# A copy of the scan inputs' PSUM tile, made by ScalarE and read by VectorE's rotations

## The chip, the cores and the metric

The kernel runs on one core of one Trainium2 chip. The metric is the device time of one execution in microseconds (us). The core's engines work side by side, each through its own queue of instructions in a fixed order: TensorE (PE; its weight loads are listed as PEld), VectorE (DVE), ScalarE (ACT), GpSimd (POOL) and SyncE (SP), which here only starts DMA transfers. Matrix products land in PSUM; everything else lies in SBUF. GpSimd has no operand in PSUM in this kernel.

## What is computed

One layer of a diffusion backbone, for 128 context tokens and 1024 latent tokens of width 1024: a normalised input goes through one input projection, whose columns feed attention (queries, keys, values) and a state-space layer (u). The part at stake is the state-space layer, a complex diagonal scan in two directions for 32 groups:

```python
bu_re = jnp.einsum('blgc,gpc->blgp', uf, bb_re)
bu_im = jnp.einsum('blgc,gpc->blgp', uf, bb_im)
bu_re = bu_re.at[:, edge].add(ab_re * h0r - ab_im * h0i)
bu_im = bu_im.at[:, edge].add(ab_re * h0i + ab_im * h0r)
_, _, h_re, h_im = lax.associative_scan(
    _complex_affine_combine, (a_re, a_im, bu_re, bu_im), axis=1, reverse=reverse)
y = (jnp.einsum('blgp,gcp->blgc', h_re, c_re[dr])
     - jnp.einsum('blgp,gcp->blgc', h_im, c_im[dr]))
```

A gated unit, the output projection and a feed-forward part follow.

## The kernel before

**Stages.** Modulation and normalisation of the input come first, to about 180 us. Then the input projection runs through 63 steps (`STEPS`), each a chunk of 256 columns for one tile of 128 tokens: 24 products of 128x256 into one tile `ps_in` (`win_mm`, L463 to L465). `ps_in` has three buffers. The step behind it empties it (`win_evac`): ScalarE with a copy (L483) or, for the queries and keys of the latent tokens, VectorE with the rotary products (L488 to L495: L488, L493 and L494 read `ps_in` in PSUM, L495 adds two SBUF tiles). VectorE also makes the low part of each weight tile (L272) behind ScalarE's cast (L271).

**The scans lie beside the projection.** The order of all instructions is written out by hand: between the products of a step, a generator (`side`) is moved on by one part, which puts instructions of the scans into all queues. `ssm_pipe` handles four groups at a time, a batch; there are eight batches (Q = 0 to 7), started some two or three steps apart, so that two or three of them overlap. In the traces they run from about 228 to 376 us.

**One batch.** Tables of sines and cosines `E` are made by ScalarE and VectorE (L926 to L959; L928 and L940 add a bias, L930, L936 and L943 are VectorE's steps between). `U` holds the transposed inputs. Then, for a direction d, `rot_in(d)`: TensorE makes the scan inputs in `pS` (L977, 16 products; one tile of two PSUM banks with a single buffer), and VectorE rotates them with the tables: `rotate` is one product of 128x576 into `tA` (L967) and two of 128x288 into `tB` (L968, L969). GpSimd adds the two into `St` (L983) and adds the start state to one column (L985). `rot_out(d)`: VectorE scans (L1001, two instructions, with the decay in `dr`, made by ScalarE at L993) into `Ht` in SBUF, rotates `Ht` back with the same `rotate`, and GpSimd adds the result into `Hp` in four instructions (L1008) and writes its edge columns (L1012 to L1018). TensorE reads `Hp` in the output products `yc` and `yl` (L1043 to L1050), two steps after the second `rot_out`.

**What sets the order around the change.** In the queue of each engine `rot_in(0)` comes one part ahead of `rot_in(1)`, and this ahead of `rot_out(0)`; `rot_out(1)` is in the part behind. With the batches interleaved, `rot_in(0)` of the next batch stands on VectorE right behind `rot_out(1)` of the one before in most batches. `tA`, `tB` and `St` have two buffers each, `pS`, `Ht` and `dr` one for their use. So the products into the next `pS` wait until the last read of the present one.

**After the scans** the projection goes on alone (TensorE), the keys are transposed, and attention begins at some 430 us.

Of the kernel before, what the change touches and what calls it, by code (L numbers as in the profile page):

```python
# [34 lines left out]
CH = 8  # L35
# [22 lines left out]
def tile_hybrid_step(  # L58
# [86 lines left out]
    def rsqrt1s(pl, cols):  # L145
        """The inverse root of some columns, divided by RS."""
        ts = []
        for ss, scale, tag in cols:
            v, y, f = [pl.tile([P, 1], F32, tag=tag + n, name=tag + n) for n in "vyf"]
            yi = pl.tile([P, 1], I32, tag=tag + "i", name=tag + "i")  # L150
            ts.append([v, y, f, yi, yi.bitcast(F32)])
        for (v, y, f, yi, cur), (ss, scale, tag) in zip(ts, cols):
            if scale is None:
                V.tensor_scalar(v, ss[:, 0:1], ss[:, 1:2], EPS, ALU.add, ALU.add)
            else:
                V.tensor_scalar(v, ss, scale, EPS, ALU.mult, ALU.add)  # L156
        for v, y, f, yi, cur in ts:
            V.tensor_single_scalar(yi, v.bitcast(I32), 1, op=ALU.logical_shift_right)
        for v, y, f, yi, cur in ts:
            V.tensor_scalar(yi, yi, -1, 0x5F3759DF, ALU.mult, ALU.add)  # L160
        for c in (-3.0, -12.0, -768.0):
            for v, y, f, yi, cur in ts:
                V.tensor_scalar(f, cur, cur, v, ALU.mult, ALU.mult)  # L163
            for x in ts:
                v, y, f, yi, cur = x
                V.scalar_tensor_tensor(y, f, c, cur, ALU.add, ALU.mult)  # L166
                x[4] = y
        return [x[1] for x in ts]
# [18 lines left out]

    # ------------------------------------------------------------- pools for the first part
    pst_es, pst = pool("pst", space=PSUM)
# [17 lines left out]

    # ------------------------------------------------------------- loads
    wm_raw = {}
# [6 lines left out]
    def load_wm0(j, n):  # L216
        """Half of a quarter of the first shift's (n even) or scale's columns."""
        if j % 2 == 0:
            w = p0.tile([P, 4, NW], F32, tag=f"x{4 + n}", name=f"wm0{j}{n}")
        else:  # L220
            if n % 2 == 0:
                wm_raw[j, n // 2] = p0w.tile([P, 2, 4, NW], F32, tag=f"w{n // 2}", name=f"wm0{j}{n}")
            w = wm_raw[j, n // 2][:, n % 2]
        wm_raw[j, n // 2, n % 2] = w
        c = n % 2 * D + j * NW
        DMA.dma_start(w, wmod[:, n // 2 * 4:n // 2 * 4 + 4, c:c + NW])
# [86 lines left out]
    load_wm0(1, 3)  # L313
    # ------------------------------------------------------------- modulation, statistics, normalised input
    def mod_mm(ps, c0, nq, k):
# [18 lines left out]

    # ------------------------------------------------------------- statistics of the rows
    TG = [(0, 4), (4, 8), (8, 9)]
# [52 lines left out]

    # ------------------------------------------------------------- input and output maps, state on the partitions  # L390
    prm = pb.tile([P, NQ, 4, 8, GC], F32, name="prm")
# [56 lines left out]

    # ------------------------------------------------------------- input projection
    u_sb = [su.tile([P, 8, CH, GC], F32, name=f"u_sb{o}") for o in range(4)]  # L450
# [53 lines left out]

    # ------------------------------------------------------------- the start

# [12 lines left out]
    def mod_out(j):  # L519
        """Shifts and scales of two blocks of channels."""  # L520
        rows = mod_rows(psm0.pop(j))
        pm = ps_t("pm0")[:, 0:P]
        PE.transpose(pm, rows, ident)
        pmv = pm.rearrange("p (i b r) -> p i r b", i=2, r=32)
        s = slice(2 * j, 2 * j + 2)
        for i, n in enumerate(("sh1", "sc1")):
            V.tensor_tensor(mods[n][:, :, s], pmv[:, i, 0:2, :],
                            bT[:, None, 8 * i + 2 * j:8 * i + 2 * j + 2].to_broadcast([P, 2, 2]), ALU.add)
        V.tensor_tensor(mods["sc1"][:, :, s], mods["sc1"][:, :, s], gT[:, 0, None, s].to_broadcast([P, 2, 2]), ALU.mult)
# [18 lines left out]

    # small things
    ones2 = pp.tile([P, 2, NS], F32, name="ones2")  # L550
# [305 lines left out]

    # ------------------------------------------------------------- maps of the scans, four groups of a direction at a time
    def after(f):
# [57 lines left out]

    # ------------------------------------------------------------- scans, four groups at a time
    def ssm_pipe(sp, Q):
# [44 lines left out]
        def tmp(n):  # L963
            return sp.tile([P, 2, 2, NS], F32, tag=n, bufs=2, name=n)
        def rotate(x, d, s):
            tA, tB = tmp("tA"), tmp("tB")
            V.tensor_mul(tA, x, tab(d, 0)[:, None].to_broadcast([P, 2, 2, NS]))  # L967
            V.tensor_mul(tB[:, s], x[:, 1 - s], tab(d, 1))  # L968
            V.scalar_tensor_tensor(tB[:, 1 - s], x[:, s], -1.0, tab(d, 1), ALU.mult, ALU.mult)  # L969
            return tA, tB  # L970
        def rot_in(d):
# [8 lines left out]
            pSv = pS[:, :, 0:2 * NS].rearrange("p r (u c) -> p r u c", u=2)  # L980
            tA, tB = rotate(pSv, d, 0)
            St = tmp("St")
            G.tensor_tensor(St, tA, tB, ALU.add)  # L983
            c0 = 0 if d == 0 else NCH - 1
# [111 lines left out]
    class Pipe:  # L1096
        """Staggered generators: a new one every `every` steps, each moved on once a step."""

# [15 lines left out]

    # the rest of the modulation, a quarter of its columns at a time
    MSEC = (2048, 3072, 4096, 5120)
# [54 lines left out]

    # ------------------------------------------------------------- keys
    kvd = {}
# [41 lines left out]

    # ------------------------------------------------------------- gated unit
    zsp = {}
# [91 lines left out]

    # ------------------------------------------------------------- the projection, with the rest beside it  # L1310
    tm_es = None
# [34 lines left out]
    p1_es.close()  # L1346
    # ------------------------------------------------------------- attention
    def rsqrt_pool(pl, ss, n, scale, tag, bufs=1, split=False):
# [188 lines left out]

    # ------------------------------------------------------------- gated unit
    gl_es, gl = pool("gl", side="left")
# [17 lines left out]

    # the context's queries go beside the unit's products
    def ctx(m):
# [117 lines left out]

    # ------------------------------------------------------------- output projection, second norm
    mx_load(order[1])
# [24 lines left out]

    # quarters of the second part's input: half of the tokens, half of its columns, half of that half of tokens
    quart = [{n: slot(f"r{4 * b + i}", dt=F32) for i, n in enumerate(("A11", "A12", "A21", "A22"))} for b in range(2)]
# [73 lines left out]

    # weights of the second part's inputs: quarters, their sums, split
    raw, wop = {}, {}
# [178 lines left out]

    # ------------------------------------------------------------- feed-forward: gate and up parts
    psf_es, psf_ = pool("psf", space=PSUM)
# [13 lines left out]
    def prod(f, i, b):  # L1977
        """One of the seven products of a block, and the sums that it completes."""
        u = un.setdefault((f, b), {})
# [125 lines left out]

    # ------------------------------------------------------------- feed-forward: second product
    HEAD = 1
# [36 lines left out]

    # the seven products of a pair of rows' tiles, of columns' halves and of token tiles (q, q + 4)
    def w2_load(p):
# [5 lines left out]
    def w2_tasks(p):  # L2152
        """Sums in place and splits: rows' tiles (0, 1), columns' halves (0, 1)."""
        at = {1: (0, 0), 7: (0, 1), 2: (1, 0), 3: (1, 1), 5: (2, 0), 6: (2, 1), 4: (1, 0)}
# [68 lines left out]
    def mm2(ps, s, p, n, ix, start, stop):  # L2223
        """Passes of one product: tokens' operand ix by the rows' operand n."""
        h, l = [t[1][:, ix] if isinstance(ix, int) else t[1][:, ix[0], ix[1]] for t in g2[s]]
        w = W2[p][n][1]
        for j, (x, y) in enumerate(((h, w[:, 0, :]), (h, w[:, 1, :]), (l, w[:, 0, :]))):
            PE.matmul(ps, x, y, start=(start and j == 0), stop=(stop and j == 2))  # L2228
# [279 lines left out]
def _rope_tables():  # L2508
    """Rotary tables of the token grid (shapes alone), rows ordered as the token tiles are:
    partition p of tile j holds token p * CH + j; the sine of an axis once for both halves."""  # L2510
    tok = (np.arange(P)[:, None] * CH + np.arange(CH)[None, :])
# [30 lines left out]
```

## Time and profile before

| what | value |
|---|---|
| median of 3 runs | 1561.93 us (1559.25 to 1562.45) |
| profiled execution, span from first to last instruction | 1562.2 us |
| TensorE busy | 1451.2 us (93%) |
| VectorE busy | 1177.3 us (75%) |
| ScalarE busy | 677.4 us (43%) |
| GpSimd busy | 534.6 us (34%) |

The profile is of one execution; its span is its own time, and only what lies ahead of the first and behind the last instruction is not in it. The page's busy shares are means over stages with different limits. The table of stretches gives the same by stage, the list of waits says which engine waited for what, and the lines of a source line give the shortest, the median and the longest duration of its instructions. Durations of neighbouring instructions of VectorE overlap a little, so that starts tell more of what one costs than ends.

### The profile page before, as it was taken

The numbers are of one execution on the slowest core, as the hardware profiler recorded it, in microseconds if no ns is written. First come the engines' busy times: TensorE is split into PE (matmuls) and PEld (weight loads), VectorE is DVE, ScalarE is ACT, GpSimd is POOL, SyncE is SP. The second block draws the span as 40 slices with busy tenths as digits, with TensorE's granted clock in tenths as the row PEclk, the third lists the DMA queues.
The fourth block names the chain that finished last, engine by engine and source line by source line (L and its number), as shares of the span: only waits on it lengthen the run. The fifth ranks groups of instructions, "written<-read, shape, count | busy, mean of one in ns | idle before, by whom it ended". The sixth has DMA issues, their size and how long they took to land. (4 is left out here: it accounts for less than half of the span.)

```text
span 1562.2 us, 27432 instructions
## 1 busy us (share of the span) xinstructions
PE 1451.2 (93%) x10331; PEld 1326.9 (85%) x10331; DVE 1177.3 (75%) x2049; ACT 677.4 (43%) x1381; POOL 534.6 (34%) x656
## 2 busy tenths in 40 slices
PE   4879998989999999989879999999999999999986
PEld 3867797888989999868779999999999996888765
DVE  5579839997558888648797666666666678898988
ACT  2443255542658887536652223222322236333322
POOL 1355417774113442321440000000000017786866
PEclk9879999999999999989999999999999999999998
DMA  9329944333442111055412222222222123333325
GB/s 294 117 80 334 338 156 120 109 114 111 126 147 80 48 49 35 8 159 166 121 42 75 81 79 72 67 82 78 72 67 81 58 94 106 107 115 106 123 94 189
DMA packets 162452, 175.70 MB, mean 112 GB/s; under 512 B 18080, under 2 KB 132720, under 8 KB 162320
## 3 DMA queue, kind: packets, MB, share of 16 engines
q1 hardware_dynamic: 161392, 173.24, 34.8%
q8 instruction: 82, 1.34, 0.4%
q10 hardware_dynamic: 816, 0.57, 0.1%
q0 software_dynamic: 112, 0.13, 0.1%
q14 instruction: 50, 0.41, 0.1%
HBM read 128.70 MB, written 45.20 MB: 111 GB/s over the span
## 5 line engine op out<-in xcount | busy, mean ns | idle before, releaser
L1984 PE MATMUL m<-l,wh 128*128 128x288 f32 x1320 | 276.7, 296 | 5.5 <-DVE l L1712 4.4
L1984 PE MATMUL m<-r,wh 128*128 128x288 f32 x1144 | 241.5, 297 | 3.4 <-DVE rav L156 3.0
L1984 PEld LDWEIGHTS m<-l,wh 128*128 128x128 f32 x1320 | 215.6, 189 | 6.6 <-DVE l L1712 4.9
L1984 PE MATMUL m<-l,wl 128*128 128x288 f32 x704 | 208.4, 296 | 2.9 <-DVE wl L1801 2.9
L1984 PEld LDWEIGHTS m<-r,wh 128*128 128x128 f32 x1144 | 188.0, 189 | 4.2 <-DVE r L1712 4.0
L463 PE MATMUL ps_in<-wh,hh 128*128 128x256 f32 x576 | 179.7, 312 | 5.0 <-DVE hh L385 4.1
L465 PE MATMUL ps_in<-wh,hl 128*128 128x256 f32 x576 | 167.4, 291 | 5.5 <-DVE hl L388 5.5
L464 PE MATMUL ps_in<-wl,hh 128*128 128x256 f32 x576 | 167.3, 290 | 0.7 <-DVE wl L272 0.7
L2162 POOL TENSOR_TENSOR l<-r 128x512 f32<-128x512 f32 x2 | 3.0, 1521 | 452.8 <-DMA r<-in_w_ffn_out_dram 452.8
L1984 PE MATMUL m<-r,wl 128*128 128x288 f32 x528 | 157.1, 298 | 0.2 <-DVE wl L1801 0.2
L1800 ACT CAST wh<-raw 128x512 fp32r<-128x512 f32 x132 | 77.8, 621 | 147.4 <-DVE raw L1826 117.6
L463 PEld LDWEIGHTS ps_in<-wh,hh 128*128 128x128 f32 x576 | 114.6, 199 | 25.3 <-issue 18.9
L1984 PEld LDWEIGHTS m<-l,wl 128*128 128x128 f32 x704 | 133.1, 189 | 3.1 <-DVE wl L1801 3.1
L1801 DVE TENSOR_TENSOR wl<-raw,wh 128x512 fp32r<-128x512 f32 x132 | 93.3, 708 | 38.5 <-ACT wh L1800 38.4
L465 PEld LDWEIGHTS ps_in<-wh,hl 128*128 128x128 f32 x576 | 114.4, 199 | 6.5 <-DVE hl L388 6.4
L464 PEld LDWEIGHTS ps_in<-wl,hh 128*128 128x128 f32 x576 | 115.0, 200 | 1.1 <-DVE wl L272 1.1
L1424 DVE TENSOR_REDUCE mx<-S 128x1 f32<-128x1152 f32 (+1 forms) x72 | 88.7, 1236 | 22.1 <-PE S L1421 21.8
L1984 PEld LDWEIGHTS m<-r,wl 128*128 128x128 f32 x528 | 100.3, 190 | 0.5 <-DVE wl L1801 0.4
L2264 DVE TENSOR_TENSOR acc<-acc,fo 128x1024 f32<-128x1024 f32 (+1 forms) x77 | 82.8, 1102 | 8.4 <-PE fo L2228 8.4
L1431 ACT ACTIVATE p<-S,mx 128x1152 f32<-128x1152 f32 (+1 forms) x72 | 81.1, 1127 | 13.9 <-DVE mx L1424 10.2
L1421 PE MATMUL S<-kT,qT 128*128 128x384 f32 x384 | 83.0, 351 | 0.5 <-ACT p L1431 0.5
L1008 POOL TENSOR_TENSOR Hp<-tA,tB 64x288 f32<-64x288 f32 x64 | 61.6, 963 | 30.7 <-DVE tB L969 26.3
(550 smaller groups left out, 3535.0 us busy)
## 6 DMA issues: line engine op xcount, KB each, us to landing
wm<-in_w_mod_dram SPq DMA_DIRECT2D x48, 512.0 KB
raw<-in_w_ffn_in_dram SPq DMA_DIRECT2D x88, 256.0 KB
g_s<-u SPq DMA_DIRECT2D x88, 144.0 KB
wraw<-in_w_in_dram SPq DMA_DIRECT2D x28, 256.0 KB
r<-in_w_ffn_out_dram SPq DMA_DIRECT2D x12, 512.0 KB
l<-in_w_ffn_out_dram SPq DMA_DIRECT2D x10, 512.0 KB
mat_s<-out SPq DMA_DIRECT2D x16, 288.0 KB
omat<-mat_s SPq DMA_DIRECT2D x8, 576.0 KB
```

Of the source, the lines that this page charges most:

```text
L463: PE.matmul(ps, la, wh, start=(k == 0), stop=False)
L464: PE.matmul(ps, la, wl, start=False, stop=False)
L465: PE.matmul(ps, lb, wh, start=False, stop=(k == KD - 1))
L1008: G.tensor_tensor(H[64 * ri:64 * ri + 64, two::2, off:off + NS], tA[s, ri], tB[s, ri], ALU.add)
L1421: PE.matmul(S[:, c, 0:cw], qT[:, 2 * h + m, j, :], K[:, 2 * h + m, c * cw:(c + 1) * cw], start=(j == 0), stop=(j == 1))
L1424: V.tensor_reduce(u["mx"][:, m:m + 1], S[:, 0:nc3, 0:cw], mybir.AxisListType.XY, ALU.max, negate=True)
L1431: A.activation(p[:, 0:nc3 * cw].rearrange("p (c n) -> p c n", n=cw), u["S"][m][:, 0:nc3, 0:cw], AF.Exp, bias=u["mx"][:, m:m + 1], scale=1. ...
L1800: A.copy(h, src)
L1801: V.tensor_sub(l, src, h)
L1984: PE.matmul(ps, w[:, k, :], a[:, k, :], start=(k == 0 and j == 0), stop=(k == 3 and j == 2))
L2162: G.tensor_tensor(x(o), x(a), x(b), ALU.subtract)
L2264: V.tensor_add(a, a, x)
```

## The change

ScalarE copies `pS` into `St` in SBUF (576 elements a partition), and the three multiplications of `rotate` read `St` instead of `pS`. GpSimd's addition then writes into the same `St`, over the copy. `rotate` itself, the scan and the back rotation are as before. Lines behind it have a number higher by one.

```diff
@@ -978,8 +978,9 @@
             pSv = pS[:, :, 0:2 * NS].rearrange("p r (u c) -> p r u c", u=2)
-            tA, tB = rotate(pSv, d, 0)
             St = tmp("St")
+            A.copy(St, pSv)
+            tA, tB = rotate(St, d, 0)
             G.tensor_tensor(St, tA, tB, ALU.add)
```

The rest of the diff takes comments away and changes no instruction. Each of the 16 calls of `rot_in` puts one instruction more into ScalarE's queue, and no other instruction is added or moved. Where it stands, in ScalarE's queue at batch 1, between the decay of batch 1 (`dr`) and the steps for the tables (`f`) and the weights (`wh`); before:

```order
L993 ACTIVATE dr_3115<-ones_293,prq 128x144 [waits DVE_49]
L993 ACTIVATE dr_3115<-ones_293,prq 128x144
L928 ACTIVATE f_3067<-f_3065,magic 128x512
L271 CAST wh<-wraw 128x512 [waits DMAHW7_49]
L940 ACTIVATE f_2904<-f_2902,magic 128x512 [waits DVE_49]
L946 COPY U<-pu 128x4x128 [waits PE_49]
```

The same place of ScalarE's queue in the changed kernel:

```order
L994 ACTIVATE dr_3117<-ones_293,prq 128x144 [waits DVE_49]
L994 ACTIVATE dr_3117<-ones_293,prq 128x144
L982 COPY St<-pS 128x576 [waits PE_49,Pool_49]
L928 ACTIVATE f_3069<-f_3067,magic 128x512
L271 CAST wh<-wraw 128x512 [waits DMAHW7_49]
L982 COPY St<-pS 128x576 [waits PE_49,Pool_49]
L940 ACTIVATE f_2904<-f_2902,magic 128x512 [waits DVE_49]
```

The two copies of the batch stand behind `dr`, which waits for VectorE's last scan of the batch before, and each waits for TensorE's products into `pS`.

On TensorE, the second direction's products into `pS` of batch 1, between products of the projection; before:

```order
L463 MATMUL ps_in<-wh,hh_3_280 128x256
L464 MATMUL ps_in<-wl,hh_3_280 128x256
L465 MATMUL ps_in<-wh,hl_3_288 128x256
L977 MATMUL pS<-U,mat 64x144 [waits DVE_49,PE_49]
L977 MATMUL pS<-U,mat 64x144 x7
```

And in the changed kernel, on TensorE at the same place:

```order
L463 MATMUL ps_in<-wh,hh_3_280 128x256
L464 MATMUL ps_in<-wl,hh_3_280 128x256
L465 MATMUL ps_in<-wh,hl_3_288 128x256
L977 MATMUL pS<-U,mat 64x144 [waits Activation_49]
L977 MATMUL pS<-U,mat 64x144 x7
```

The order is the same; the products now wait for ScalarE's copy of the first direction's `pS` instead of VectorE's three reads of it. On VectorE the order is the same too, and `pS` as the first operand of L967 to L969 has become `St`.

## Rows read from the trace of the kernel before

**Rows 1.** The page, busy time: engine, us, share of the span, instructions.
```profile
PE 1451.2 (93%) x10331; PEld 1326.9 (85%) x10331; DVE 1177.3 (75%) x2049; ACT 677.4 (43%) x1381; POOL 534.6 (34%) x656
```

**Rows 2.** Busy time by stretch: us, engines, granted clock, DMA share, GB/s.
```profile
240.00:360.00 120.00, 101.95 (x970) 93.77 (x969) 114.94 (x192) 56.48 (x143) 87.49 (x123) 0.94 0.41 118
...
376.00:424.00 48.00, 47.58 (x417) 47.41 (x418) 24.65 (x62) 25.82 (x46) 4.08 (x4) 1.00 0.42 126
```

**Rows 3.** Waits, 200 to 400 us: total, times, longest one.
```profile
PE pS L977 <- DVE tB L969: 18.1, 7, 4.6
...
ACT dr L993 <- DVE Ht L1001: 12.2, 4, 4.5
...
DVE Ht L1001 <- POOL St L985: 2.6, 4, 0.7
...
DVE tA L967 <- PE pS L977: 2.2, 2, 1.5
```

**Rows 4.** Timeline of TensorE, VectorE and GpSimd at the last batch: start, duration, instruction.
```profile
357.81 1.27 PE L977 MATMUL pS<-U,mat 128*64 128x144 f32 x16 [2.48 <-DVE tB L969]
...
375.30 0.66 PE L1043 MATMUL yc<-omat,Hp 128*32 128x128 f32 x16
...
359.19 0.76 DVE L967 TENSOR_TENSOR tA<-pS,E 128x576 f32<-128x576 f32 x1 [1.53 <-PE pS L977]
...
370.50 3.80 POOL L1008 TENSOR_TENSOR Hp<-tA,tB 64x288 f32<-64x288 f32 x4 [0.47 <-DVE tB L969]
...
375.30 0.19 POOL L1018 COPY Hp<-h0s 128x4 f32<-128x4 f32 x1
```

**Rows 5.** Line L967: shortest, median, longest in ns; first and last start.
```profile
L967 DVE TENSOR_TENSOR tA<-pS,E x16: 744/748/758, 228.4 to 359.2; 128x576 f32<-128x576 f32 x16
L967 DVE TENSOR_TENSOR tA<-Ht,E x16: 757/758/1185, 236.7 to 368.4; 128x576 f32<-128x576 f32 x16
```

**Rows 6.** Line L946, ScalarE's copy out of PSUM, 226 to 372 us.
```profile
L946 ACT COPY U<-pu x7: 559/585/588, 230.1 to 341.8; 128x512 f32<-128x512 f32 x7
```

**Rows 7.** Lines L488, L495, L930 and L1008, 226 to 372 us.
```profile
L488 DVE TENSOR_TENSOR rt<-ps_in,rc x18: 409/411/420, 238.7 to 370.9; 128x256 f32<-128x256 f32 x18
...
L495 DVE TENSOR_TENSOR st<-st,rt x18: 424/1028/1053, 239.6 to 371.7; 128x256 f32<-128x256 f32 x18
...
L930 DVE SCALAR_TENSOR_TENSOR f<-f,f x6: 685/686/1289, 238.1 to 335.1; 128x512 f32<-128x512 f32 x6
...
L1008 POOL TENSOR_TENSOR Hp<-tA,tB x62: 784/886/1190, 238.3 to 371.7; 64x288 f32<-64x288 f32 x62
```

**Rows 8.** Timeline of VectorE and GpSimd, 292 to 297 us.
```profile
292.99 1.29 DVE L930 SCALAR_TENSOR_TENSOR f<-f,f 128x512 f32<-128x512 f32 x1
294.20 1.28 DVE L272 TENSOR_TENSOR wl<-wraw,wh 128x512 fp32r<-128x512 f32 x1
...
292.62 4.40 POOL L1008 TENSOR_TENSOR Hp<-tA,tB 64x288 f32<-64x288 f32 x4 [2.32 <-DVE tB L969]
```

**Rows 9.** Timeline of VectorE and GpSimd at 230 us.
```profile
230.26 1.75 DVE L943 SCALAR_TENSOR_TENSOR f<-f,f 128x512 f32<-128x512 f32 x1 [0.37 <-ACT f L940]
...
230.03 1.43 POOL L983 TENSOR_TENSOR St<-tA,tB 128x576 f32<-128x576 f32 x1 [13.63 <-ACT dr L993]
```

**Rows 10.** Timeline of VectorE and GpSimd at batch 3, 282 to 289 us.
```profile
282.06 0.75 DVE L967 TENSOR_TENSOR tA<-pS,E 128x576 f32<-128x576 f32 x1
...
283.45 1.03 DVE L936 TENSOR_TENSOR f<-f,f 128x512 f32<-128x512 f32 x1
...
285.25 1.03 DVE L495 TENSOR_TENSOR st<-st,rt 128x256 f32<-128x256 f32 x1
...
282.29 3.70 POOL L1008 TENSOR_TENSOR Hp<-tA,tB 64x288 f32<-64x288 f32 x4 [1.69 <-DVE tB L969]
...
286.58 1.42 POOL L983 TENSOR_TENSOR St<-tA,tB 128x576 f32<-128x576 f32 x1
```

**Rows 11.** Busy time of 358 to 362 us, columns as in rows 2.
```profile
358.00:362.00 4.00, 4.00 (x30) 3.73 (x28) 2.81 (x5) 0.00 (x0) 3.15 (x5) 0.60 0.42 135
```

## The prediction

> **What bounds the kernel now.** I read the page first: TensorE is busy for 93% of the span, so a change in work that VectorE and ScalarE do beside it is worth what it moves on TensorE, in its own stage [rows 1]. The scans run from about 228 to 376 us. There the table of stretches turns the picture round: between 240 and 360 us VectorE is busy for 114.9 of 120 us, TensorE for 102.0, ScalarE for 56.5, at a granted clock of 0.94; from 376 us on TensorE is busy for 47.6 of 48 and VectorE for 24.7 [rows 2]. So in the scans VectorE is late, behind them TensorE is.
>
> The list of waits says how the two hang together: seven times, 18.1 us in all, TensorE waits before the products into pS until VectorE has written tB, its last read of the pS before [rows 3]. pS has one buffer, and these are the only long waits of TensorE there. This is what the change goes for.
>
> The question is whether those 18.1 us reach the end. I followed the last batch. TensorE's output product of the eighth batch (yc, L1043) begins to take Hp at 375.30; GpSimd's last copy into that Hp starts at 375.30 and lasts 0.19; no wait is listed [rows 4]. The two arrive together, and behind that point TensorE has no gap. GpSimd's Hp follows from VectorE's last rotation (0.47 us idle until tB) [rows 4], and that from VectorE's queue, which is full. So the end moves with **VectorE's chain through the eight batches**: a TensorE that is early at the last yc only waits there. Long before, it waits elsewhere: ps_in has three buffers, which VectorE empties (L488 to L494) at fixed places of the same full queue.
>
> **The change part by part.** Removed: the 48 reads of pS by VectorE (three for each of 16 tiles). The three instructions themselves stay, in the same places. From pS tA takes 744 to 758 ns; the same instruction on Ht, which lies in SBUF, takes 757 ns at least and 758 at the median [rows 5]. For VectorE the copy is no lighter work: zero for 48 instructions, a few tenths of a us at most on the wrong side. The Trainium skill (VectorE: DVE Perf Modes, "The TRN2 errata") gives a VectorE instruction a fixed 58 cycles from SBUF and 120 from PSUM, at 0.96 GHz; by it 48 instructions would gain an estimated 3.1 us and the forecast would be 1570. The rows on the two forms of tA show none of that, so it is left out of the sum.
>
> Added on ScalarE: 16 copies of 128x576. The nearest row is its copy of 128x512 from PSUM, 585 ns [rows 6]; by elements about 0.65 us. ScalarE has half of its time free, so 10.5 us of copies are hidden, except where a copy stands between TensorE and a waiting VectorE. Behind a copy in ScalarE's queue are the bias steps of the tables (L928, L940) and the weight casts (L271), which VectorE takes up later. In batches 1, 3, 4 and 5 the first copy stands right behind the activation of dr, which itself waits for VectorE's last scan (ACT dr on Ht: 4 times, 12.2 us) [rows 3]; VectorE has three rotation instructions to do after that scan, about as long as dr and copy together, so nothing is added there. In batch 0 VectorE isn't full and waits for pS itself (2.2 us in two waits, 1.53 of them at the last batch, so 0.7 here) [rows 3, 4]: copy and hand-over come on top, **+0.8 us**.
>
> Added on VectorE, by what it now reads: **waiting for GpSimd**. The trace shows two kinds of VectorE instruction. Those with one operand in PSUM don't notice GpSimd: L488 takes 409 to 420 ns in all 18 cases [rows 7]. Those with both operands in SBUF do: L495 takes 424 ns at best and 1028 at the median; L930 and L272 right behind each other, both while GpSimd adds up Hp, take 1.29 and 1.28 us [rows 7, 8], where the least for L930 is 0.69 [rows 7]. So each instruction that meets the Hp additions is held by 0.6 us, also several in a row. Beside the longer addition of St it is 1.06: L943 takes 1.75 us there [rows 9] against a usual 0.69. The rotations of pS are of the first kind, and after the change of the second. That rotations on Ht look unharmed is because GpSimd is mostly waiting for their tB; the one that meets GpSimd takes 1185 ns, 0.43 over the median [rows 5].
>
> Batch 3 shows the place. The first direction's rotation starts at 282.06, the four Hp additions at 282.29, and until 285.99 they run beside it, L936 and L495; L936 now takes 0.34 more than the 0.69 of L930, which has its size, and L495 0.61 more than its least, 0.95 of holding in all [rows 7, 10]. After: tA starts first and is free, the two tB and L936 are held 0.6 each, and L495 meets the rest of the fourth addition, 0.2 or so: 2.0. Net +1.1. Batches 1 to 7 all have the rotation beside such additions, some with more of them left, some with less: 7 x 1.1 = **+7.7 us**. The bounds are zero (no hold) and three full holds each, 7 x 1.8 = 12.6.
>
> The second direction's rotation runs beside the addition of St (in batch 3 from 286.58 on, 1.42 us [rows 10]), and in four batches the scan behind it then waits for that St, 2.6 us in all, 0.65 each [rows 3]. One hold of 1.06 takes the place of such a wait: +0.4, four times: **+1.6 us**. In batch 7 VectorE now waits 1.53 us for pS [rows 4]; TensorE will no longer be late there, and a hold of 1.06 comes instead: **-0.5 us**. VectorE's chain: 0.8 + 7.7 + 1.6 - 0.5 = **+9.6 us**.
>
> **What TensorE makes of it.** Its waits move rather than go: VectorE's chain gets longer, TensorE's work doesn't, so it waits more than now, at ps_in and before the last yc. There is one effect behind that. After the wait of 2.48 us at 357.81 the clock granted is 0.60 in the 4 us from 358 [rows 4, 11], so most of that at the lower level (1.2 GHz): 0.4 x 4 = 1.6 us lost. Today that loss lies ahead of the tie at 375 us. After the change the last long wait is the one at the yc itself (I expect some 3 us, between the emptying of ps_in and Hp), and the loss lies behind it, on the path: **+1.6 us**. From there on TensorE's work is as before, without gaps that could take up a shift of 10 us.
>
> Sum: 9.6 + 1.6 = 11.2 us on the span of 1562.2, so 1573.4; the median of the runs, 1561.93, is the same as that span within 0.3. I forecast 1573.
>
> **The rivals.**
> 1. *The hold takes the whole instruction of GpSimd*, not 0.6 us: 0.89 (median of an Hp addition [rows 7]) and 1.42 for St [rows 10]. Then three holds for each first direction are longer by 0.29, 7 x (1.1 + 0.87) = 13.8 instead of 7.7, and five of the second by 0.36, 1.8: 7.9 us over the forecast, 1581. Against it: consecutive holds of 0.60. The Trainium skill says this (SBUF, "Who interferes with whom"): VectorE with two SBUF inputs and a GpSimd instruction that reads SBUF exclude each other, and the second waits until the first has finished. The rows agree on who is hit, not on how much. 5%.
> 2. *No hold that matters*: the rotations find gaps in GpSimd's work, or the delays fall where VectorE would have waited. Then 0.8 - 1.5 on VectorE's chain and up to 1.6 of clock: 1562 to 1564, no difference. For it: rotations on Ht are nearly all at 758 ns. 15%.
> 3. *TensorE's waits do set the end*, and the change does what it is written for: faster. All 18.1 us would give 1544. But VectorE's queue allows only its own idle time to go: 2.6 us of waits for St and 1.5 for pS [rows 3, 4], so 1558. It decides if the holds stay under those 4.1 us and batch 7 gains from an early pS. For it: the clock, 0.94 in the stage, would recover too. 9%.
> 4. *ScalarE's queue stalls VectorE*: a copy that waits for pS keeps L928, L940 or the casts back. With the 0.65 us of a copy in each of 16 places, 10 us on top: 1584. Against it: ScalarE's idle half. 3%.
>
> **How the numbers follow.** The forecast has the remaining 68%; with its bounds (holds half as large or a third larger, clock loss or none) it runs from 1566 to 1579. A range of 1561 to 1581 takes in the first and the second rival, and leaves out the third and the fourth. Slower by over 0.2% (3.1 us, about what a measurement of this kernel can tell from no change): forecast, first and fourth rival, 0.76. Faster by as much: most of the third, 0.08. The rest within it, 0.16.
>
> **What would show it.** In the profile after: tA and tB from St up to 1.3 and 1.0 us where they meet Hp, at 0.76 and 0.45 elsewhere; the wait of TensorE for tB gone from pS, and waits of the same size at ps_in (on VectorE's L494) or at yc (on GpSimd's Hp); VectorE still over 95% busy in the stage, and that stage some 10 us longer; the copies at 0.6 to 0.7 us; a granted clock near 0.5 behind the last yc. I am wrong if tA from St stays at 0.76 beside GpSimd, or if the last yc comes before 376 us.

## The result and the profile after

The changed kernel takes **1573.01 us** (median, 1572.08 to 1574.73), the kernel before 1561.56 beside it: a ratio of 1.0079, 95% interval 1.0064 to 1.0093. The forecast was 1573, slower. The profiled execution took 1574.73 us with a span of 1573.0, 10.8 us more than before. In the changed kernel the copy is L982; the lines behind it have moved down by one.

The page's busy times answer to [rows 1]: VectorE has 11 us more, ScalarE 9 (the copies), GpSimd 9 (7.4 of them in its additions and small copies beside the scans; the last section comes back to this).

```profile
PE 1455.7 (93%) x10331; PEld 1330.0 (85%) x10331; DVE 1188.3 (76%) x2049; ACT 686.7 (44%) x1397; POOL 543.2 (35%) x656
```

The same stretches as in [rows 2], with the end of the scans apart (columns: us; busy us of TensorE, its weight loads, VectorE, ScalarE, GpSimd; granted clock, DMA share, GB/s):

```profile
240.00:360.00 120.00, 101.47 (x915) 91.66 (x915) 118.91 (x178) 60.11 (x148) 87.06 (x111) 0.90 0.35 104
371.00:386.00 15.00, 10.36 (x102) 9.62 (x100) 14.72 (x27) 1.79 (x4) 11.73 (x16) 0.93 0.36 103
386.00:436.00 50.00, 49.58 (x420) 49.19 (x413) 24.45 (x62) 25.82 (x46) 4.08 (x4) 0.95 0.40 121
384.00:388.00 4.00, 2.36 (x16) 1.98 (x17) 2.44 (x6) 0.00 (x0) 1.42 (x4) 0.50 0.57 176
388.00:392.00 4.00, 4.00 (x26) 4.00 (x26) 0.00 (x0) 0.65 (x2) 0.00 (x0) 0.66 0.02 5
```

VectorE had 5 of 120 us free between 240 and 360; now it has 1. It also does less in them: 178 instructions instead of 192. Behind the scans, from 386 us on, TensorE is full again, but around the last wait, from 384 to 392 us, the granted clock is 0.50 and then 0.66.

The waits from 200 to 420 us, as in [rows 3]:

```profile
ACT dr L994 <- DVE Ht L1002: 17.9, 6, 6.3
...
PE pS L977 <- ACT St L982: 13.8, 5, 4.9
...
PE yc L1044 <- POOL Hp L1019: 6.2, 5, 2.1
...
PE ps_in L463 <- DVE st L494: 2.5, 1, 2.5
```

TensorE's 18.1 us of waits for VectorE's tB are gone by name, but 13.8 us of them have come back as waits for the copy. The first line says why: in ScalarE's queue the copy stands behind dr, and dr waits for VectorE's scan. To these come 6.2 us before yc and 2.5 before ps_in.

What VectorE pays is seen by adding up its instructions from the first rotation to the last Hp, with the same counts in both kernels. These groups are of the kernel before, 228.30 to 375.60 us (busy us and mean ns, then idle time ahead of the group):

```profile
L967 DVE TENSOR_TENSOR tA<-pS,E 128x576 f32<-128x576 f32 x16 | 12.0, 749 | 2.9 <-PE pS L977 2.2 <-ACT E L990 0.7
...
L969 DVE SCALAR_TENSOR_TENSOR tB<-pS,E 128x288 f32<-128x288 f32 x16 | 7.1, 446 | 0.0
L968 DVE TENSOR_TENSOR tB<-pS,E 128x288 f32<-128x288 f32 x16 | 7.1, 445 | 0.0
```

And these of the changed kernel, 229.60 to 385.65 us:

```profile
L967 DVE TENSOR_TENSOR tA<-St,E 128x576 f32<-128x576 f32 x16 | 14.5, 905 | 3.6 <-DMA wraw<-in_w_in_dram 2.5 <-ACT St L982 1.1
...
L969 DVE SCALAR_TENSOR_TENSOR tB<-St,E 128x288 f32<-128x288 f32 x16 | 12.1, 754 | 0.0
L968 DVE TENSOR_TENSOR tB<-St,E 128x288 f32<-128x288 f32 x16 | 12.0, 749 | 0.0
L272 DVE TENSOR_TENSOR wl<-wraw,wh 128x512 fp32r<-128x512 f32 x10 | 11.7, 1166 | 0.0
```

The 48 rotation instructions grew from 26.2 to 38.6 us, **+12.4** with rounding. The others take a part of it back: L272 10.5 to 11.7, L936 5.1 to 5.9, L943 5.9 to 5.4, L495 18.0 to 17.1, the scans' waits for St 2.6 to 0.2, together -1.8; and inside the stretch VectorE waits 1.1 us ahead of tA instead of 2.2, and no more the 0.4 us ahead of L943. From the first rotation to the last copy into Hp it is 155.6 us (229.75 to 385.39) instead of 146.9 (228.40 to 375.30).

Batch 3 shows how it happens; timeline of VectorE and GpSimd in the changed kernel, the place of [rows 10]:

```profile
284.62 0.75 DVE L967 TENSOR_TENSOR tA<-St,E 128x576 f32<-128x576 f32 x1
285.29 1.05 DVE L968 TENSOR_TENSOR tB<-St,E 128x288 f32<-128x288 f32 x1
286.26 1.05 DVE L969 SCALAR_TENSOR_TENSOR tB<-St,E 128x288 f32<-128x288 f32 x1
...
290.66 1.68 DVE L969 SCALAR_TENSOR_TENSOR tB<-St,E 128x288 f32<-128x288 f32 x1
...
284.84 4.34 POOL L1009 TENSOR_TENSOR Hp<-tA,tB 64x288 f32<-64x288 f32 x4 [1.69 <-DVE tB L969]
...
290.38 1.65 POOL L984 TENSOR_TENSOR St<-tA,tB 128x576 f32<-128x576 f32 x1
```

tA has started before GpSimd and runs at 0.75. Both tB start beside the Hp additions and take 1.05 instead of 0.45. In the second direction one tB meets the St addition and takes 1.68. In the other batches it is the same: tA at 1.35, tB at 1.05 beside Hp, 1.66 or 1.68 beside St, everything else at 0.75 to 0.80 and 0.44 to 0.47.

The end, in the timeline of TensorE and GpSimd, as [rows 4]:

```profile
381.98 0.35 PE L463 MATMUL ps_in<-wh,hh 128*128 128x256 f32 x1 [2.50 <-DVE st L494]
...
385.64 0.66 PE L1044 MATMUL yc<-omat,Hp 128*32 128x128 f32 x8 [2.14 <-POOL Hp L1019]
...
385.39 0.19 POOL L1019 COPY Hp<-h0s 128x4 f32<-128x4 f32 x1
```

The last copy into Hp starts 10.1 us later than the 375.30 of before, and TensorE, which was there on time, now waits for it. Such a difference of two times on the clock takes in where the scans began: the first products into pS end at 227.61 here, at 228.02 before, and anywhere between 222.97 and 228.02 in the ten profiles, though the code up to them is the same. Lengths from the first rotation on are free of that, and are used below.

### The profile page after: what moved, and what is told of

It is laid out like the page before. It is cut to its first block, busy times and chain, and to the rows that moved or that the text cites. A ratio compares the mean times of both kernels' runs of the same rounds, so it can differ in the third digit from the quotient of the medians.

```text
span 1573.0 us, 27458 instructions
## 1 busy us (share of the span) xinstructions
PE 1455.7 (93%) x10331; PEld 1330.0 (85%) x10331; DVE 1188.3 (76%) x2049; ACT 686.7 (44%) x1397; POOL 543.2 (35%) x656
## 5 line engine op out<-in xcount | busy, mean ns | idle before, releaser
L464 PE MATMUL ps_in<-wl,hh 128*128 128x256 f32 x576 | 166.3, 289 | 0.5 <-DVE wl L272 0.3
L463 PEld LDWEIGHTS ps_in<-wh,hh 128*128 128x128 f32 x576 | 113.7, 197 | 27.7 <-issue 21.4
L1802 DVE TENSOR_TENSOR wl<-raw,wh 128x512 fp32r<-128x512 f32 x132 | 93.4, 709 | 38.6 <-ACT wh L1801 38.5
L464 PEld LDWEIGHTS ps_in<-wl,hh 128*128 128x128 f32 x576 | 113.9, 198 | 0.9 <-DVE wl L272 0.9
L1425 DVE TENSOR_REDUCE mx<-S 128x1 f32<-128x1152 f32 (+1 forms) x72 | 88.6, 1236 | 22.0 <-PE S L1422 21.6
L2265 DVE TENSOR_TENSOR acc<-acc,fo 128x1024 f32<-128x1024 f32 (+1 forms) x77 | 82.8, 1102 | 9.2 <-PE fo L2229 9.2
L1432 ACT ACTIVATE p<-S,mx 128x1152 f32<-128x1152 f32 (+1 forms) x72 | 81.1, 1127 | 13.8 <-DVE mx L1425 10.2
```

Source lines behind the costliest of these rows:

```text
L463: PE.matmul(ps, la, wh, start=(k == 0), stop=False)
L464: PE.matmul(ps, la, wl, start=False, stop=False)
L1425: V.tensor_reduce(u["mx"][:, m:m + 1], S[:, 0:nc3, 0:cw], mybir.AxisListType.XY, ALU.max, negate=True)
L1432: A.activation(p[:, 0:nc3 * cw].rearrange("p (c n) -> p c n", n=cw), u["S"][m][:, 0:nc3, 0:cw], AF.Exp, bias=u["mx"][:, m:m + 1], scale=1. ...
L1802: V.tensor_sub(l, src, h)
L2265: V.tensor_add(a, a, x)
```

## The experiments

The **theory**: VectorE's chain sets the end of the scans, and the rotations got slower because both operands now lie in SBUF while GpSimd reads SBUF too. The **rivals**: the price is the copy itself, by ScalarE's queue or by a longer way from TensorE to VectorE; or TensorE's own waits set the end.

**The copies made, but not read.** The copy goes into St, the rotations read pS.

```diff
             St = tmp("St")
-            tA, tB = rotate(pSv, d, 0)
+            A.copy(St, pSv)
+            tA, tB = rotate(pSv, d, 0)
```

> The 16 copies of pS into St are made as in the changed kernel, but the rotations read pS as before (the copy is overwritten unread). Theory (the time comes from GpSimd holding VectorE's multiplications once both their operands lie in SBUF): 1560 to 1564, no different from before, tA and tB at 0.75 and 0.45 us everywhere, last Hp written at 375 to 376 us. Rival A (the copies themselves: ScalarE's queue and the hand-over delay VectorE's chain): 1568 or more. Rival B (an SBUF operand is slower for VectorE, GpSimd or not) gives 1562 as well and is told apart by the next two.

Measured: 1562.93 us, ratio 1.0008 (0.9996 to 1.0019), no difference, as expected; the kernel before takes 1561.31 beside it and beside the next three. From the first rotation to the last copy into Hp it is 147.5 us (227.16 to 374.68). The rotations stay at means of 753 and 446 ns. The first one waits for the copy here too, though it reads pS: 2.48 us, as in the changed kernel, until 0.03 us behind the copy's end. So 16 copies in ScalarE's queue, hand-over included, cost nothing that can be measured; the interval leaves room for 3 us.

**Only tA reads the copy**, both tB read pS.

```diff
-        def rotate(x, d, s):
+        def rotate(x, d, s, xa=None):
+            xa = x if xa is None else xa
...
-            V.tensor_mul(tA, x, tab(d, 0)[:, None].to_broadcast([P, 2, 2, NS]))
+            V.tensor_mul(tA, xa, tab(d, 0)[:, None].to_broadcast([P, 2, 2, NS]))
...
-            tA, tB = rotate(pSv, d, 0)
+            A.copy(St, pSv)
+            tA, tB = rotate(pSv, d, 0, St)
```

> Only tA reads the copy, the two tB read pS: one of three multiplications can be held, and VectorE waits for the copy as in the changed kernel. Theory: in the changed kernel tA is on average 0.16 us longer than from pS and each tB 0.30, so 16 x 0.16 = 2.5 us and 0.8 of hand-over, 1564 to 1567. Rival A (copies and hand-over): 1573, as with all three. Rival B: a third of the 11 us, spread over all 16 tA evenly (each 0.2 longer, GpSimd busy or not), 1565.

Measured: 1572.28 us, ratio 1.0059 (1.0036 to 1.0082). That is nearly the whole loss with only 4 holds, and was not what the theory expected. VectorE's groups, 227.60 to 382.05 us:

```profile
L1003 DVE TENSOR_TENSOR_SCAN Ht<-dr,St 128x288 f32<-128x288 f32 x32 | 37.8, 1220 | 5.0 <-POOL St L987 5.0
...
L968 DVE TENSOR_TENSOR tA<-St,E 128x576 f32<-128x576 f32 x16 | 14.4, 902 | 8.6 <-ACT St L983 7.2 <-POOL Hp L1010 1.4
```

The holds of tA are 2.4 us (902 against 749 ns). The larger part is idle time: 8.6 us ahead of tA and 5.0 ahead of the scans, where before had 2.9 and 2.6. Ahead of tA: here pS is freed only by the last tB, so the copy of the second direction starts late, and tA waits for TensorE and ScalarE one after the other: 2.50 us at the last batch alone, where before waits 1.53. Ahead of the scans: the four waits for St are twice as long (1.25 to 1.27 each). The second direction of batch 4, in the kernel before and in this one:

```profile
304.54 0.74 DVE L967 TENSOR_TENSOR tA<-pS,E 128x576 f32<-128x576 f32 x1
304.54 0.19 POOL L1017 COPY fin<-Hp 128x4 f32<-128x4 f32 x1
...
304.93 1.43 POOL L983 TENSOR_TENSOR St<-tA,tB 128x576 f32<-128x576 f32 x1
```

```profile
306.86 0.75 DVE L968 TENSOR_TENSOR tA<-St,E 128x576 f32<-128x576 f32 x1
306.86 0.79 POOL L1019 COPY fin<-Hp 128x4 f32<-128x4 f32 x1
...
307.85 1.42 POOL L985 TENSOR_TENSOR St<-tA,tB 128x576 f32<-128x576 f32 x1
```

Beside a tA that reads pS, GpSimd's small copy takes 0.19 us; beside one that reads St it takes 0.79, and the addition into St follows 0.99 us behind tA instead of 0.39. In the other three batches it is the same: the addition comes 0.6 us later, and the scan waits for it. So the hold goes both ways: here VectorE holds GpSimd, and pays at its next wait. The rival on the longer way was right **for this variant** as to the idle time ahead of tA, not as to that ahead of the scans. In the changed kernel the copy itself frees pS, and behind the first rotation tA waits 1.1 us for it in the whole stage. (The 2.5 us that stand with a DMA in its row are the wait ahead of the first rotation; in the other kernels with a copy the same 2.5 us stand with the copy.)

**Only the two tB read the copy**, tA reads pS: the same edit, with the two sources exchanged.

```diff
-            tA, tB = rotate(pSv, d, 0)
+            A.copy(St, pSv)
+            tA, tB = rotate(St, d, 0, pSv)
```

> The two tB read the copy, tA reads pS (so pS is released after copy and tA). Theory: 32 x 0.30 = 9.6 us less what other instructions are then spared, 1569 to 1573; tB at 0.45 where GpSimd is idle and at 1.05 or more beside its additions, nothing between. Rival A: 1562 to 1564 if the copy is ready by the time tA is done, for its hand-over is then hidden. Rival B: two thirds of 11 us, all tB a little longer, 1569.

Measured: 1565.71 us, ratio 1.0025 (1.001 to 1.0039), less than expected. Four of the 32 tB take 0.60 to 0.68 us, which the expectation had excluded. VectorE's groups, 227.30 to 377.45 us:

```profile
L1003 DVE TENSOR_TENSOR_SCAN Ht<-dr,St 128x288 f32<-128x288 f32 x32 | 37.7, 1216 | 0.0
L495 DVE TENSOR_TENSOR st<-st,rt 128x256 f32<-128x256 f32 x19 | 16.8, 884 | 0.7
...
L970 DVE SCALAR_TENSOR_TENSOR tB<-St,E 128x288 f32<-128x288 f32 x16 | 10.8, 675 | 0.0
L969 DVE TENSOR_TENSOR tB<-St,E 128x288 f32<-128x288 f32 x16 | 10.8, 673 | 0.0
```

The tB are held 7.4 us (21.6 against 14.2), but the scans wait no more for St (2.6 us saved), L495 meets fewer additions (1.2 saved), and the stretch as a whole is 2.9 us longer than before, 150.2 against 147.3. A hold is paid only where VectorE would not have waited, or been held, at once behind it.

**Less work for TensorE.** The product L464 is left out of the convolution in the steps that run beside the scans, some 21 us of TensorE's work; the projection lacks that term there.

```diff
-            PE.matmul(ps, la, wl, start=False, stop=False)
+            if not less:
+                PE.matmul(ps, la, wl, start=False, stop=False)
...
-        mm = win_mm(c0, t)
+        mm = win_mm(c0, t, less=27 <= s < 49)
```

> The kernel before, with the middle one of the three products of each k (wl by hh, L464) left out in the 22 steps of the projection that run beside the scans (steps 27 to 48): some 21 us of TensorE's work less, all of it ahead of the last yc. Theory (VectorE's chain sets the end of the scans, TensorE's waits there are worth nothing): the last Hp stays at 375 within 1.5 us, TensorE waits longer by what it is spared, 1560 to 1565 (up to 2.5 us of a lower clock behind the last wait). Rival (TensorE's work and its waits for pS set the end): 1541 to 1546.

Measured: 1561.66 us, ratio 0.9997 (0.9981 to 1.0013). TensorE's waits from 200 to 420 us:

```profile
PE pS L978 <- DVE tB L970: 28.2, 7, 6.7
PE yc L1044 <- POOL Hp L1019: 2.1, 1, 2.1
```

From the first rotation to the last copy into Hp it is 146.8 us (225.95 to 372.78), as before. Over the scans TensorE is idle for 32.7 of 147.3 us instead of 18.4, 10 us of the difference at pS; the rest of the 21 us goes into its other products, at a granted clock of 0.87 instead of 0.94. In this stage its time is worth nothing.

**GpSimd's additions into Hp cut to 8 of 288 columns**, in the kernel before and in the changed one, run together. What the rest of Hp would carry is left out, so only differences between the two count.

```diff
+            G.memset(H, 0.0)
...
-                    G.tensor_tensor(H[64 * ri:64 * ri + 64, two::2, off:off + NS],
-                                    tA[s, ri], tB[s, ri], ALU.add)
+                    G.tensor_tensor(H[64 * ri:64 * ri + 64, two::2, off:off + 8],
+                                    tA[s, ri, :, 0:8], tB[s, ri, :, 0:8], ALU.add)
```

> The kernel before with GpSimd's four additions into Hp cut to 8 of their 288 columns and Hp cleared first (the rest of Hp is zero, so what the scan gives back is left out nearly whole). GpSimd then hardly reads SBUF beside VectorE, but for the additions into St. Theory (VectorE is held beside GpSimd's additions, and its chain sets the end): VectorE's other two-input instructions in the scan run at their unheld times, L495 from a mean of about 947 ns toward 430 (19 of them, up to 10 us), L272 from 1046 toward 690 (10 of them, up to 3.6 us), the last addition's 3 us fall away; together 8 to 15 us faster than before, 1547 to 1553, unless TensorE's own work comes to bind. Rival (what the changed kernel pays is the price of an operand read from SBUF or of ScalarE's copy by itself, not of GpSimd's reads): the same gain here, so this run is the partner that the next is measured against.

> The changed kernel with the same cut of GpSimd's additions into Hp. Theory: the holds of the first direction's rotations (8.4 us of the 12.1 in the changed kernel's trace) are gone, the ones beside the additions into St stay (3.7 us, against 2.6 us of waits that they replace), and the first copy's hand-over stays (about 1.4 us): 2 to 4 us slower than e4_short_before. Rival: 9 to 11 us slower than e4_short_before, as after is than before.

Measured: 1543.12 us with pS read by VectorE (ratio 0.9881, 0.9863 to 0.9899) and 1540.98 with the copy (0.9872, 0.9852 to 0.9891), beside 1560.92 for the kernel before. Both gain more than the 1547 to 1553 that was expected of the first. The loss of 11 us is gone; the intervals of the two overlap. From the first rotation to the last copy into Hp it is 125.8 us in the one (223.35 to 349.10) and 125.0 in the other (227.24 to 352.22), where the full kernels have 146.9 and 155.6. VectorE's groups of the changed kernel with the cut, 227.20 to 364.00 us:

```profile
L1002 DVE TENSOR_TENSOR_SCAN Ht<-dr,St 128x288 f32<-128x288 f32 x32 | 31.8, 1033 | 0.0
L967 DVE TENSOR_TENSOR tA<-St,E 128x576 f32<-128x576 f32 x16 | 13.1, 816 | 4.5 <-ACT St L982 4.5
...
L968 DVE TENSOR_TENSOR tB<-St,E 128x288 f32<-128x288 f32 x16 | 7.3, 455 | 0.0
L969 DVE SCALAR_TENSOR_TENSOR tB<-St,E 128x288 f32<-128x288 f32 x16 | 7.3, 454 | 0.0
```

tB reads the same copy from the same place and takes 455 ns instead of 749 to 754; tA has one hold of 1.0 us left, beside an St addition. So it is not the reading of SBUF that costs, but GpSimd reading it at the same time. Two things make the loss vanish here, and this pair alone does not part them: the holds are gone (27.7 us of rotations instead of 38.6), and VectorE is no longer what the end waits for. TensorE's waits for pS are down to 4.5 and 3.9 us, and in the twenty microseconds around the last Hp it shows no gap and a granted clock of 1.00. The order of the two came out against the theory, which wanted the copy 2 to 4 us slower.

**The evacuation's product in PSUM.** rt (L485) goes into the unused half of the PSUM tile that it is made from. L488 then writes PSUM and L495 has one operand there. Nothing is left out. In the kernel before, and in the changed one:

```diff
-               ps1.tile([P, 512], F32, tag="mm", bufs=3, name="ps_in"))[:, 0:NW]
+               ps1.tile([P, 512], F32, tag="mm", bufs=3, name="ps_in"))
+        full, ps = ps, ps[:, 0:NW]
...
-            t1 = p1c.tile([P, NW], F32, tag="rt", bufs=1, name="rt")
+            t1 = full[:, NW:2 * NW]
```

> The kernel before, where the product rt of the convolution's evacuation (L488) goes into the unused half of the PSUM tile it is made from and not into SBUF, so that the addition L495 has one operand in PSUM. Theory (only instructions with two operands in SBUF are held): L495 falls from a mean of about 947 ns toward 430 in the scan, up to 9 us off VectorE's chain there; with what TensorE's later release of the tile costs, 3 to 9 us faster than before, 1552 to 1558. Rival (the hold goes by what else VectorE touches, for example its output in SBUF, or TensorE's waits set the end): no change within 0.2%, 1559 to 1564.

> The changed kernel with rt in PSUM in the same way. Theory: 3 to 9 us faster than the changed kernel (1564 to 1570), and still 8 to 12 us slower than e6_before_rt_psum, since the rotations are held as before. Rival: no change against the changed kernel, 1571 to 1575.

Measured: 1555.48 us (ratio 0.9962, 0.9948 to 0.9977) and 1565.27 us (1.0026, 1.0013 to 1.004; single runs from 1559.58 to 1569.54). The first is **faster than both kernels**, by 5.4 us; the second is 9.8 slower than it, as the theory expected, and faster than the changed kernel by its ratio (1.0026 against 1.0079, intervals apart). The addition (L497 there) and the instructions that now meet GpSimd in its place, 227.30 to 369.10 us of the first:

```profile
L969 DVE TENSOR_TENSOR tA<-Ht,E 128x576 f32<-128x576 f32 x16 | 13.4, 838 | 0.5
...
L272 DVE TENSOR_TENSOR wl<-wraw,wh 128x512 fp32r<-128x512 f32 x10 | 11.0, 1102 | 0.0
...
L497 DVE TENSOR_TENSOR st<-st,ps_in 128x256 f32<-128x256 f32 x19 | 8.0, 421 | 0.7
```

The addition falls from a mean of 947 to 421 ns, 10.0 us in 19 instructions. Other instructions take 1.7 us of that back (tA on Ht 785 to 838 ns, L272 1046 to 1102, L938, the former L936, 851 to 918), and the stretch is 5.5 us shorter, 141.8 against 147.3. From the first rotation to the last copy into Hp it is 141.5 us (227.33 to 368.87) instead of 146.9. This is the mirror image of the change: an operand moved out of SBUF takes its instruction out of the holds, as one moved in puts it there.

## Why the prediction was right

**What sets the end.** As put: with TensorE relieved of 21 us the scans took as long as before and so did the kernel, and with VectorE's stretch shorter by 5.5 us the kernel gained 5.4. The last Hp and the last yc moved together.

**The removed reads at zero.** Right: where the rotations meet nothing, tA takes 744 to 760 ns from pS and from St alike. The gain that the Trainium skill gives an operand in SBUF over one in PSUM (VectorE: DVE Perf Modes, "The TRN2 errata") is not seen here: tA from St 0.75, tB 0.45, as from pS.

**ScalarE's copies at zero, but for batch 0.** Right on the queue (the unread copies cost nothing clear of noise). In batch 0 the hand-over was mis-sized, and something else made up for it. The kernel before, then the changed one:

```profile
226.82 1.20 PE L977 MATMUL pS<-U,mat 128*64 128x144 f32 x16
...
228.40 0.76 DVE L967 TENSOR_TENSOR tA<-pS,E 128x576 f32<-128x576 f32 x1 [0.73 <-ACT E L990]
```

```profile
226.41 1.20 PE L977 MATMUL pS<-U,mat 128*64 128x144 f32 x16
...
229.10 0.62 ACT L982 COPY St<-pS 128x576 f32<-128x576 f32 x1
...
229.75 0.76 DVE L967 TENSOR_TENSOR tA<-St,E 128x576 f32<-128x576 f32 x1 [2.48 <-DMA wraw<-in_w_in_dram]
```

The first rotation starts 2.1 us behind the end of its products instead of 0.4: the copy stands behind four activations of dr in ScalarE's queue, which take 1.33 us from 227.87 on. The second direction waits 0.4 us longer. But L943 no longer waits 0.4 us and no longer meets the addition into St (0.68 us at 231.16 instead of the 1.75 of [rows 9]). At its first scan VectorE is only 0.3 us later than before (234.41 against 234.09), 0.7 reckoned from the end of the products. The term was 0.8.

**The holds.** The 0.6 us were right to the hundredth, and so was what is hit. The term was mis-sized: 7.7 us forecast, 10.3 measured from the first direction's rotation to the second's in batches 1 to 7. Of these 8.4 are 14 holds of the rotations (0.6 to 1.8 us a batch); the other 1.9 are neighbours that now meet more of GpSimd's additions (L272 in batch 6 1.88 us instead of 0.68, L943 in batch 4 1.28 instead of 0.76). The Trainium skill (SBUF — State Buffer, "Who interferes with whom") calls what VectorE and GpSimd share an exclusive lock, for which a VectorE instruction with two SBUF inputs contends with a GpSimd instruction that reads SBUF. The runs agree on which are hit: L488, with a PSUM operand, stays at 414 ns. They nearly agree on the size. An addition into Hp that meets nothing of VectorE's takes 0.79 us (four in the kernel before), and the hold beside one is 0.60; an addition into St that meets nothing takes 1.41 to 1.43, and the longest hold beside one is 1.23. Both are 0.2 us short of the whole instruction.

**The second direction.** Here even the sign was wrong: +1.6 and -0.5 were forecast, -0.5 in all was measured. Only three batches (3, 5 and 7) had a hold there, 3.7 us, and against them stand 2.4 us of waits for St and the 1.5 us for pS that went. In batches 1 and 4 VectorE came late enough to meet nothing, and lost its wait for St as well.

VectorE's chain in all: 0.3 + 10.3 - 0.5 = 10.1, by which the last Hp moved. The forecast of 9.6 is so near because three errors, -0.5, +2.6 and -1.6, nearly cancel; that is luck.

**TensorE's waits.** "Gone from pS" was wrong. I counted the copy's wait behind dr as harmless because VectorE has as long to do; for VectorE it is harmless, but TensorE waits for the copy too, and 13.8 of the 18.1 us stayed at pS under another name. It cost nothing, since TensorE is not late there.

**The clock.** As put in place and cause: low at 0.50 and 0.66 around and behind the last yc, after waits of 2.50 and 2.14 us. It was mis-sized: the first product behind the scans' output (pz) came 12.5 us later than before (394.02 against 381.56), the last Hp 10.1, so 2.4 us instead of 1.6. The two rows, before and after:

```profile
381.56 1.03 PE L1068 MATMUL pz<-ident,u_sb 128*128 128x128 f32 x8
```

```profile
394.02 1.04 PE L1069 MATMUL pz<-ident,u_sb 128*128 128x128 f32 x8
```

TensorE then stays 12.5 us late until 423 us and 11.7 to 11.8 from there to 660; behind that the shift goes up and down in steps between 8.6 and 12.9, and the span ends 10.8 longer. I forecast no such thing, and no run settled what moves it there. So the sum of 11.2 is near the 10.8 partly by chance.

**The rivals.** TensorE's waits as the end and a stalled ScalarE are refuted above, by TensorE's lighter work and by the unread copies; no hold that matters, by the 12.1 us of holds in the rotations. The whole instruction as the hold failed by its price: it took 0.89 us for an addition into Hp, the median of additions many of which were themselves held, and a tB would then take 1.33 and not 1.05. In kind it was nearly right.

**The range.** The inner bounds do not give the 1579 of its upper end: holds a third larger add some 3 us to 1573, and three full holds everywhere 4.9. The wider range and the chances do not rest on it.

## What to carry to other kernels

A copy from PSUM to SBUF "to free the bank" also moves an operand. If the reader is VectorE and its other operand is in SBUF, it joins the instructions that GpSimd's additions hold back, and that hold GpSimd back, so look first what GpSimd does beside it; and look whether the waiting engine is late at all. The other way round is cheap to try where a VectorE product has spare room in its own PSUM tile: leave it there (10.0 us of instruction time, 5.4 us of the whole here).

## What the runs showed of the hardware

Two things I had not expected. First, the scans are held as well: the pair (L1002) takes 2.57 to 2.60 us where an addition into St runs beside it, 1.99 to 2.57 where additions into Hp do (0.7 us of them, or 1.9 and more), and 1.39 where neither does. With the additions into Hp cut short, the pairs beside them take 1.39 to 1.42, and the mean of a scan falls from 1218 to 1033 ns. Second, a GpSimd instruction that only writes SBUF holds nothing. Timeline of VectorE and GpSimd in the changed kernel with short Hp additions:

```profile
306.84 1.64 DVE L495 TENSOR_TENSOR st<-st,rt 128x256 f32<-128x256 f32 x1
...
309.81 2.57 DVE L1002 TENSOR_TENSOR_SCAN Ht<-dr,St 128x288 f32<-128x288 f32 x2
312.41 0.76 DVE L967 TENSOR_TENSOR tA<-Ht,E 128x576 f32<-128x576 f32 x1
...
306.75 1.44 POOL L984 TENSOR_TENSOR St<-tA,tB 128x576 f32<-128x576 f32 x1
...
310.03 1.73 POOL L984 TENSOR_TENSOR St<-tA,tB 128x576 f32<-128x576 f32 x1 [1.49 <-DVE tB L969]
...
312.31 0.57 POOL L1005 MEMSET Hp<- 128x580 f32 x1
```

L495 starts beside an addition and takes 1.64 us instead of 0.42; the scan takes 2.57; tA runs beside the memset for half a microsecond and takes its usual 0.76, and four pairs of scans lie beside 0.58 us of such a memset and still take 1.40. The addition that starts first ends at its 1.44, the one that starts inside a scan takes 1.73: GpSimd is held as well, as its small copy was above. In the changed kernel its busy time beside the scans is 7.4 us longer than before.
